# Strassen's algorithm for the feed-forward products, and modulation sums on the matmul engine, in a two-layer diffusion step

## The chip, the cores and the metric

One core of one Trainium2 chip runs the whole step as one program. The metric is the device time of a run in microseconds (us); the median of several runs is compared. Engines are named as the profile names them: PE is TensorE (matmuls), PEld its weight loads, DVE is VectorE, ACT is ScalarE, POOL is GpSimd and SP is SyncE, on whose queue this kernel issues all its DMA transfers.

## The reference, cut to what matters

Two layers work on 1152 tokens (1024 latent tokens and 128 context tokens) of 1024 features, all in float32. Each layer is a mixer (layer 0: a recurrence beside a pooling mixer, layer 1: latent attention) and then a feed-forward block. Ahead of both stands an RMS norm that is modulated with a scale and a shift from the conditioning vectors. The change concerns the feed-forward block and the modulation:

```python
def sq_relu_mlp(h, w1, w2):
    return jnp.square(jax.nn.relu(h @ w1)) @ w2      # 1024 -> 4096 -> 1024

m = jax.nn.silu(cond) @ w_mod + b_mod                # 1024 -> 6 * 1024, per layer and token kind
h = rms_norm(x, g) * (1 + scale) + shift
x = x + gate * sq_relu_mlp(h, w1, w2)
```

## The kernel before, in words

Activations lie feature-major: 128 features on the partitions, tokens along the free dimension. The 1152 tokens form three chunks of 384 (`CH`); the last holds the end of the latent tokens and the context tokens, which have their own modulation, so that vector operations on it come in two pieces (256 and 128 columns, `groups`, L236).

Float32 products keep their accuracy by splitting. `split` (L143) makes a rounded high part of an operand on ACT and the remainder, a subtraction, on DVE or POOL; `mm3` (L151 to L154) then issues three matmuls for each pair of tiles: high by high, high by low, low by high.

The feed-forward block is `ffn` (L707). It walks over 16 blocks of 256 hidden features. For each block two units of w1 and two of w2 (128 by 1024, 512 KB each) are loaded into `w_raw` by SP and split by ACT and DVE. `up` (L715) computes 2 x 128 hidden features of one chunk through `project` (L338, 24 matmuls into one PSUM bank), takes the relu on ACT (L719), the square on ACT for its high part and once more on POOL (L723), and the low part on DVE (L724). `down` (L729) multiplies with w2: for each of 8 output tiles 6 matmuls, and then DVE adds the bank, times the gate, to the activations `x` (`accum`, L335). A layer's block so issues 16 x 3 x 2 x 24 = 2304 matmuls in `up` and 16 x 3 x 8 x 6 = 2304 in `down`, each of 384 columns. In the last block `Tail` (L314) follows the additions with the squares and sums of the next norm, whose statistics (`Norm.stat`, L256) PE computes between other products, when `tick` (L302) says so.

During the feed-forward block of layer 0 the modulation of layer 1 is computed by `mod_slow` (L203), 384 of its 6144 columns at a time, in 16 parts: DVE multiplies rows of the weights by the conditioning and sums them up (L212, L214), PE adds over the partitions (L219) and transposes (L225). Layer 0's own modulation goes by `mod_steps` (L178), where PE does the products (L186): two matmuls of 512 columns for each slice of 128 rows, in a column group of the array of their own.

The order of PE's work is the order in which the program is written; all other engines and the DMA queue get theirs from a planner, except in the attention. A PSUM bank is one of eight that rotate (`bank`, L121). A buffer in a pool is handed on when its last reader is done. Attention, between the two feed-forward blocks, is computed head by head, and the change leaves it as it is.

## Time and profile before

| | |
|---|---|
| median of 3 runs | 2982.24 us (2981.44 to 2993.78) |
| span of the profiled execution | 2983.0 us |
| PE busy | 2838.5 us, 95% |
| DVE, ACT, POOL busy | 1868.8, 1130.8, 644.5 us |
| DMA | 188.22 MB, 63 GB/s on average |

The profiled execution is an execution of its own; only its span is given, and what lies around it is not listed. Busy time of PE is the union of its matmuls, which are pipelined: one of 384 columns is drawn 0.33 us long, yet the next starts long before it ends. The pace of PE is therefore read from start to start. A row of a timeline gives the start and the length in us, the engine, the line, and what is written from what.

### The profile page before, as it was taken

How to read it: one execution, taken by the hardware profiler on the slowest of the kernel's cores; microseconds unless marked ns; L12 is line 12 of the kernel's file. 1: busy time of each engine (PE TensorE's matmuls, PEld its weight loads, DVE VectorE, ACT ScalarE, POOL GpSimd, SP SyncE). 2: the span in 40 equal slices, each digit the busy share in tenths (PEclk: the TensorE clock that was granted, in tenths of full speed). 3: DMA queues.
4: the chain of work that ended last, by engine and by line, in shares of the span. 5: the costliest groups of instructions: out<-in, count | busy, mean ns of one | idle time of the engine just before them, and what ended most of it. 6: DMA issues, size and time to landing. Idle time of an engine off the chain costs nothing.

```text
span 2983.0 us, 43431 instructions
## 1 busy us (share of the span) xinstructions
PE 2838.5 (95%) x16896; PEld 2742.9 (92%) x16896; DVE 1868.8 (63%) x3400; ACT 1130.8 (38%) x2490; POOL 644.5 (22%) x600
## 2 busy tenths in 40 slices
PE   6898799999999999998999999999999999999997
PEld 3886699999999999988999999988999999999997
DVE  5469667776666666475777777775754454535355
ACT  3256333112121211255777777773521212121214
POOL 3444131001010100234323333340400101010003
PEclk7999899999999999999999999999999999999998
DMA  5233402222121222120000000023211111111101
GB/s 224 81 131 103 167 22 84 80 91 85 60 80 59 80 69 72 51 79 21 21 13 21 14 15 22 16 100 124 79 43 43 43 43 43 36 44 36 50 15 64
DMA packets 73415, 188.22 MB, mean 63 GB/s; under 512 B 9481, under 2 KB 40057, under 8 KB 72057
## 3 DMA queue, kind: packets, MB, share of 16 engines
q1 hardware_dynamic: 73208, 185.45, 18.3%
q8 instruction: 133, 2.18, 0.3%
q14 instruction: 74, 0.60, 0.1%
HBM read 168.67 MB, written 16.74 MB: 62 GB/s over the span
## 4 chain that ended last, share of the span: by engine, by line
PE 47%; ACT 3%; DVE 3%; issue 1%; DMA 1%; POOL 1%; SPq 0%; DVEq 0%; ACTq 0%; POOLq 0%
PE ps_b L152 10%; PE ps_b L153 10%; PE ps_b L154 10%; PE pS_o L978 3%; PE pS_t L960 3%; PE pS_s L152 3%; PE pS_s L154 2%; PE pS_s L153 2%; ACT aw_p L953 1%; PE pS_g L152 1%; PE pS_g L154 1%; PE pS_g L153 1%; ACT aw_ph L964 1%; DVE aw_mx L943 1%; DVE nt_xn L292 0%
## 5 line engine op out<-in xcount | busy, mean ns | idle before, releaser
L335 DVE SCALAR_TENSOR_TENSOR x_t<-ps_b,const_t,x_t 128x384 f32<-128x384 f32 (+2 forms) x1152 | 560.8, 513 | 274.9 <-PE ps_b L154 272.7
L152 PE MATMUL ps_b<-ffn_ah,wl_hlh 128*128 128x384 f32 x1488 | 498.5, 335 | 0.0
L154 PE MATMUL ps_b<-ffn_ah,wl_hll 128*128 128x384 f32 x1488 | 498.0, 335 | 0.0
L153 PE MATMUL ps_b<-ffn_al,wl_hlh 128*128 128x384 f32 x1488 | 497.9, 335 | 0.0
L723 POOL TENSOR_TENSOR ffn_r<-ffn_r 128x768 f32<-128x768 f32 x96 | 147.5, 1537 | 1437.6 <-ACT ffn_ah L722 1225.3
L148 ACT ACTIVATE wl_hlh<-w_raw 128x1024 fp32r<-128x1024 f32 x89 | 91.2, 1054 | 704.5 <-PE ps_b L153 694.8
L154 PEld LDWEIGHTS ps_b<-ffn_ah,wl_hll 128*128 128x128 f32 x1488 | 279.8, 188 | 0.0
L152 PEld LDWEIGHTS ps_b<-ffn_ah,wl_hlh 128*128 128x128 f32 x1488 | 279.8, 188 | 0.0
L153 PEld LDWEIGHTS ps_b<-ffn_al,wl_hlh 128*128 128x128 f32 x1488 | 279.8, 188 | 0.0
L719 ACT ACTIVATE ffn_r<-ps_b 128x384 f32<-128x384 f32 x192 | 93.1, 485 | 432.4 <-PE ps_b L154 432.1
L968 DVE TENSOR_TENSOR aw_pl<-pS_t,aw_ph 128x384 fp32r<-128x384 f32 (+1 forms) x400 | 200.2, 540 | 84.4 <-ACT aw_ph L964 78.8
L724 DVE TENSOR_TENSOR ffn_al<-ffn_r,ffn_ah 128x768 fp32r<-128x768 f32 x96 | 92.5, 963 | 243.3 <-POOL ffn_r L723 243.3
L953 ACT ACTIVATE aw_p<-pS_s,aw_nb 128x384 f32<-128x384 f32 (+1 forms) x400 | 224.6, 578 | 14.7 <-DVE aw_nb L947 14.0
L943 DVE TENSOR_REDUCE aw_mx<-pS_s 128x1 f32<-128x384 f32 (+1 forms) x400 | 203.2, 538 | 30.6 <-PE pS_s L154 29.5
L964 ACT ACTIVATE aw_ph<-pS_t 128x384 fp32r<-128x384 f32 (+1 forms) x400 | 173.6, 486 | 83.9 <-PE pS_t L960 83.5
L214 DVE SCALAR_TENSOR_TENSOR nt_acc<-nt_sq,const_t,nt_acc 128x384 f32<-128x384 f32 x224 | 160.9, 757 | 31.7 <-DMA nt_sq<-in_w_mod 30.2
L152 PE MATMUL ps_b<-ht0a_t,fw_w1h 128*128 128x384 f32 x480 | 164.0, 342 | 0.0
L152 PE MATMUL ps_b<-ht_t,fw_w1h 128*128 128x384 f32 x480 | 163.7, 341 | 0.0
L154 PE MATMUL ps_b<-ht0a_t,fw_w1l 128*128 128x384 f32 x480 | 162.6, 339 | 0.0
L152 PE MATMUL ps_b<-ht2a_h,fw_w1h 128*128 128x384 f32 x480 | 162.5, 339 | 0.0
L153 PE MATMUL ps_b<-ht2a_h,fw_w1h 128*128 128x384 f32 x480 | 162.5, 339 | 0.0
L154 PE MATMUL ps_b<-ht2a_h,fw_w1l 128*128 128x384 f32 x480 | 162.5, 339 | 0.0
(348 smaller groups left out, 6732.1 us busy)
## 6 DMA issues: line engine op xcount, KB each, us to landing
w_raw<-in_ffn SPq DMA_DIRECT2D x64, 512.0 KB, 4.3
w_raw<-in_l_ffn_w SPq DMA_DIRECT2D x64, 512.0 KB, 3.2
nt_sq<-in_w_mod SPq DMA_DIRECT2D x128, 192.0 KB, 2.4
w_raw<-in_w_mod SPq DMA_DIRECT2D x32, 512.0 KB, 3.8
w_raw<-in_w_in SPq DMA_DIRECT2D x18, 512.0 KB, 5.2
start_raw<-in_w_mod SPq DMA_DIRECT2D x16, 512.0 KB, 10.9
w_raw<-in_l_w_out SPq DMA_DIRECT2D x16, 512.0 KB, 4.1
n_t<-in_x SPq DMA_DIRECT2D x3, 1536.0 KB
```

The source lines that it names most:

```text
L152: mm(out, wh, hh, start=start, stop=False)
L153: mm(out, wh, hl, start=False, stop=False)
L154: mm(out, wl, hh, start=False, stop=stop)
L214: ve.scalar_tensor_tensor(acc[q], raw, sil[:, k, q:q + 1], acc[q], op0=OP.mult, op1=OP.add)
L335: done = ve.scalar_tensor_tensor(xv, b[:, a + o:e + o], gate[:, m, g:g + 1], xv, op0=OP.mult, op1=OP.add)
L719: act(r[:, j, :], b[:, :CH], AF.Relu)
L723: po.tensor_tensor(r, r, r, op=OP.mult)
L724: ve.tensor_tensor(al, r, ah.bitcast(F32), op=OP.subtract)
L943: ve.tensor_reduce(self.mx[:, i:i + 1], self.sc[i][0], axis=AX.X, op=OP.max)
L953: act(self.pt[i][:, :w], v, AF.Exp, bias=self.nb, accum_out=lsum[:, self.h, self.blk, i:i + 1])
L964: act(hi[g][:, :self.nks[g], j * P:(j + 1) * P], self.tp[g], AF.Copy)
L968: ve.tensor_tensor(lo[g][s_], self.tp[g], hi[g][s_].bitcast(F32), op=OP.subtract)
```

## The change

The tokens form four chunks of 288 (`Q`) from the output projection of layer 0 on (the attention's own blocks stay). Both feed-forward products are computed by one level of Strassen's algorithm in the form with seven products: token chunks in pairs (`g`, two pairs), features in halves. Seven right sides (`hp`: three of the activations themselves and four sums, slots 0 to 6) stand once for each pair in SBUF. For each of the 16 blocks the seven left sides come from four 128 x 512 quarters of the weights (`left_sides`, four subtractions or additions on POOL, in place, then seven splits). `up` issues for each of the seven products 4 x 3 matmuls of 288 columns, and combines the seven banks into four results with DVE, ACT and POOL; they are squared by one DVE operation. The squared results go to DRAM, three of them split (`ad`) and all four raw (`ar`).

Then the second product: blocks 0 and 1 (`PLAIN`) are multiplied as before, without Strassen, at two places where the activations change. The other 14 go in seven pairs; each product, chunk pair and output tile has 6 matmuls of 288 columns, and DVE adds the bank to an accumulator in SBUF. Right sides 0 to 2 are loaded from `ad` into three rotating buffers (`at`); 3 to 6 are summed by POOL from `ar` and split by ACT and DVE. At the end `collect` combines the accumulators, and `gated` adds them to `x`.

`mod_slow` goes. Layer 1's modulation is computed by `mod_steps` on PE, two slices after every fourth product of `up` in layer 0 (`mod_aside`). The norms and the output projection run over chunks of 288; some buffers are laid out anew.

```diff
+Q = 288
+NQ = T // Q
+PRODUCTS = (("A11", 0), ("S3", 5), ("A22", 4), ("S2", 3), ("A12", 1), ("S1", 6), ("S4", 2))
+LATE = (("A11", 0), ("A12", 1), ("S3", 5), ("A22", 4), ("S2", 3), ("S1", 6), ("S4", 2))
+PLAIN = (0, 1)
...
-    def mod_slow(l, r, s):
...
+    def enter(l, g, hp, scope):
+        hi, lo = hp
+        for k in range(4):
+            a = scope.t([P, 4, Q], tag="ac", bufs=2)
+            for j in range(2):
+                c = 2 * g + j
+                for i in range(2):
+                    kk = k + 4 * i
+                    for p, e, q in groups(c):
+                        r = a[:, PLACE[i, j], p:e]
+                        ve.scalar_tensor_tensor(r, x[c][:, kk, p:e], sc_ffn[l][:, kk, q:q + 1], nm.rs[c][:, p:e],
+                                                op0=OP.mult, op1=OP.mult)
+                        act(r, r, AF.Identity, bias=mod[l][:, 24 + kk, q:q + 1])
+            split(hi[:, 0:3, k, :], lo[:, 0:3, k, :], a[:, 0:3, :])
+            right_sides(a.unsqueeze(1))
+            split(hi[:, 3:7, k, :], lo[:, 3:7, k, :], a, eng=(ve, po)[k % 2])
+
+    def right_sides(a):
+        for o, p, q, op in ((2, 2, 3, OP.subtract), (3, 3, 0, OP.subtract), (0, 2, 0, OP.add), (1, 1, 0, OP.subtract)):
+            po.tensor_tensor(a[:, :, o, :], a[:, :, p, :], a[:, :, q, :], op=op)
+
+    def left_sides(quads, slots, low, order=PRODUCTS):
+        sub = lambda o, p, q, op=OP.subtract: po.tensor_tensor(o, p, q, op=op)
+        for name, _ in order:
+            out = []
+            for i, (a11, a12, a21, a22) in enumerate(quads):
...
+                h, lo = next(slots)
+                split(h, lo, src, eng=po if (name, i) in low else ve)
+                out.append((h, lo))
+            yield out
...
+    UP_LOW = {("A12", 0), ("S1", 0)}
+    DOWN_LOW = {(n, 1) for n, _ in PRODUCTS} | {("A12", 0), ("S4", 0)}
...
+        def up(g, s, cw):
+            a = fu.t([P, 6, Q], tag="ac", bufs=2)
+            place = lambda i: a[:, i, :]
+            bk = {}
+            for name, o in PRODUCTS:
+                (wh, wl), = next(cw)
+                b = bk[name] = bank()[:, :Q]
+                for k in range(4):
+                    mm3(b, wh[:, k * P:(k + 1) * P], wl[:, k * P:(k + 1) * P], hp[0][:, o, k, :], hp[1][:, o, k, :],
+                        k == 0, k == 3)
+                tick(1.5)
+                aside(fq)
+                plus = lambda e, to, p, q: e.tensor_tensor(place(to), p, place(q), op=OP.add)
+                if name == "A11":
+                    act(place(3), b, AF.Copy)
+                if name == "S2":
+                    plus(ve, 4, b, 3)
+                    plus(ve, 5, bk["S3"], 4)
+                    plus(ve, 1, bk["A22"], 5)
+                if name == "A12":
+                    plus(ve, 0, b, 3)
+                if name == "S1":
+                    act(place(2), b, AF.Copy)
+                    plus(po, 4, place(4), 2)
+                    plus(po, 2, place(5), 2)
+                if name == "S4":
+                    plus(ve, 3, b, 4)
+            ve.scalar_tensor_tensor(a[:, 0:4, :], a[:, 0:4, :], 0.0, a[:, 0:4, :], op0=OP.max, op1=OP.mult)
+            for p, e in ((0, 3), (3, 4)) if s in PLAIN else ((0, 3),):
+                t = fu.t([P, 3, 2, Q], F32R, tag="ah", bufs=2)[:, :e - p]
+                split(t[:, :, 0, :], t[:, :, 1, :], a[:, p:e, :])
+                nc.sync.dma_start(ad[s, g][:, p:e], t.bitcast(F32))
+            if s not in PLAIN:
+                nc.sync.dma_start(ar[s, g], a[:, 0:4, :])
...
+        for g in range(2):
+            if g:
+                enter(l, 1, hp, fu)
+                plain(0, raws, cycle(four(fq)), True, False)
+            for s in range(ns):
...
+                    cw = left_sides([up_quad(l, s, raws)], slots, UP_LOW)
+                up(g, s, cw)
...
+        for s in todo[::2]:
...
+            for name, o in LATE:
+                ws = next(cw)
+                for g in range(2):
+                    t = next(ats)
+                    if o > 2:
+                        n = 2 // len(right[g])
+                        for i, b in enumerate(right[g]):
+                            split(t[:, i * n:i * n + n, 0, :], t[:, i * n:i * n + n, 1, :],
+                                  b[:, :, o - 3, :])
+                    else:
+                        nc.sync.dma_start(t.bitcast(F32), ad[s:s + 2, g, :, o, :, :].rearrange("s p h q -> p s h q"))
+                    for m in range(4):
+                        b = bank()[:, :Q]
+                        for j in range(2):
+                            mm3(b, ws[j][0][:, m * P:(m + 1) * P], ws[j][1][:, m * P:(m + 1) * P],
+                                t[:, j, 0, :], t[:, j, 1, :], j == 0, j == 1)
...
+                            ve.tensor_tensor(to, b, to, op=OP.add)
+                    if end:
+                        collect(name, g)
...
+        plain(1, raws, ats, False, True)
...
+    def mod_aside(mq):
+        nonlocal count
+        count += 1
+        if count % 4:
+            return
+        s_ = next(mods1, None)
+        if s_:
+            if s_[0] not in mg1:
+                mg1[s_[0]] = mod_steps(1, s_[0], mq, 3)
+            next(mg1[s_[0]])
+            if s_[1] < KT // 2:
+                next(mg1[s_[0]])
```

## Rows read from the trace of the kernel before

**Rows 1.** The page: busy us of each engine, share of the span, instructions.

```profile
PE 2838.5 (95%) x16896; PEld 2742.9 (92%) x16896; DVE 1868.8 (63%) x3400; ACT 1130.8 (38%) x2490; POOL 644.5 (22%) x600
```

**Rows 2.** Windows over both feed-forward stretches: busy us of each engine, clock, DMA share, GB/s.

```profile
468.00:1289.00 821.00, 814.88 (x4650) 799.04 (x4650) 550.96 (x947) 169.07 (x258) 95.22 (x65) 1.00 0.22 73
2169.00:2961.00 792.00, 790.99 (x4526) 790.67 (x4526) 371.01 (x645) 165.48 (x249) 83.93 (x61) 1.00 0.11 39
```

**Rows 3.** Timeline of PE, layer 0 feed-forward: start, length; 68 matmuls of 384 columns apart.

```profile
900.04 0.33 PE L152 MATMUL ps_b<-ffn_ah,wl_hlh 128*128 128x384 f32 x1
...
911.83 0.33 PE L154 MATMUL ps_b<-ffn_ah,wl_hll 128*128 128x384 f32 x1
```

**Rows 4.** Timeline of PE, value projections: 23 matmuls of 256 columns apart.

```profile
1375.59 0.28 PE L152 MATMUL ps_b<-wkv_wkvh,kv_t 128*128 128x256 f32 x1
...
1378.35 0.27 PE L154 MATMUL ps_b<-wkv_wkvh,kv_t 128*128 128x256 f32 x1
```

**Rows 5.** Groups of DVE: line, form, count | busy us, mean ns | idle before.

```profile
L724 DVE TENSOR_TENSOR ffn_al<-ffn_r,ffn_ah 128x768 fp32r<-128x768 f32 x96 | 92.5, 963 | 243.3 <-POOL ffn_r L723 243.3
...
L506 DVE SCALAR_TENSOR_TENSOR ring_r<-ring_r,ring_r 128x1160 f32<-128x1160 f32 x8 | 10.6, 1352 | 0.0
...
L149 DVE TENSOR_TENSOR slots_wgl<-w_raw,slots_wgh 128x512 fp32r<-128x512 f32 x5 | 3.4, 682 | 3.9 <-ACT slots_wgh L148 3.9
```

**Rows 6.** Groups of POOL, as in group 5.

```profile
L149 POOL TENSOR_TENSOR att_t<-aw_qf,att_t 64x256 fp32r<-64x256 f32 x70 | 49.9, 730 | 0.0
L149 POOL TENSOR_TENSOR aw_ql<-aw_qf,aw_qh 128x384 fp32r<-128x384 f32 x47 | 47.4, 1008 | 194.6 <-ACT aw_qh L148 160.2 <-DMA dram_t<-aw_o 34.5
...
L884 POOL TENSOR_TENSOR aw_v<-vr_vr,aw_v 128x640 fp32r<-128x640 f32 x16 | 25.1, 1573 | 1.2
```

**Rows 7.** Source views of two DVE lines: ns min/median/max, first and last start.

```profile
L968 DVE TENSOR_TENSOR aw_pl<-pS_t,aw_ph x400: 272/548/559, 1404.5 to 2031.8; 128x384 fp32r<-128x384 f32 x128, 128x128 fp32r<-128x128 f32 x6
...
L1273 DVE TENSOR_TENSOR x_t<-x_t,nt_rs x16: 543/548/1371, 2946.0 to 2978.9; 128x384 f32<-128x384 f32 x16
```

**Rows 8.** Window over the attention, as in group 2.

```profile
1430.00:1940.00 510.00, 498.66 (x3578) 481.04 (x3576) 374.44 (x876) 387.43 (x1148) 167.54 (x213) 1.00 0.06 18
```

**Rows 9.** Timeline of DVE and POOL behind the last products.

```profile
2963.71 7.33 POOL L1273 TENSOR_TENSOR x_t<-x_t,nt_rs 128x384 f32<-128x384 f32 x6 [5.04 <-DVE nt_acc L254]
...
2965.04 2.61 DVE L1273 TENSOR_TENSOR x_t<-x_t,nt_rs 128x384 f32<-128x384 f32 x2
...
2967.58 2.61 DVE L254 TENSOR_TENSOR nt_acc<-nt_acc,nt_sq 128x384 f32<-128x384 f32 x2
```

**Rows 10.** Groups of ACT, as in group 5.

```profile
L719 ACT ACTIVATE ffn_r<-ps_b 128x384 f32<-128x384 f32 x192 | 93.1, 485 | 432.4 <-PE ps_b L154 432.1
L148 ACT ACTIVATE wl_hlh<-w_raw 128x1024 fp32r<-128x1024 f32 x89 | 91.2, 1054 | 704.5 <-PE ps_b L153 694.8 <-DMA w_raw<-in_w_in 8.9 <-DMA w_raw<-in_l_w_out 0.9
```

**Rows 11.** Timeline of PE around two slices of the layer 0 modulation.

```profile
204.98 0.34 PE L154 MATMUL ps_b<-ht_t,wl_hll 128*128 128x384 f32 x1
205.25 1.04 PE L186 MATMUL ps_b<-w_raw,const_t 128*2 128x512 f32 x8
206.22 0.44 PE L152 MATMUL ps_b<-slots_xh,slots_wgh 128*128 128x384 f32 x1
```

**Rows 12.** Groups of PE: sums and transposes of the layer 1 modulation.

```profile
L219 PE MATMUL ps_b<-nt_acc,const_t 128*2 128x384 f32 x64 | 13.0, 484 | 0.0
...
L225 PE MATMUL ps_b<-const_t,nt_rs 128*128 128x128 f32 x48 | 8.0, 275 | 2.0 <-ACT nt_rs L221 2.0
```

**Rows 13.** DMA issues: count, size, median us from issue to landing.

```profile
w_raw<-in_ffn SPq DMA_DIRECT2D x64, 512.0 KB, 4.3
w_raw<-in_l_ffn_w SPq DMA_DIRECT2D x64, 512.0 KB, 3.2
```

**Rows 14.** Window over the start, as in group 2.

```profile
0.00:30.00 30.00, 16.06 (x58) 2.95 (x62) 10.05 (x46) 8.79 (x16) 5.89 (x22) 0.85 0.94 364
```

More of the change, by code (lines that the diff above doesn't have):

```diff
@@ L628, in emit, with out_proj @@
     ht.close()
-    sw = Each("wo", "right")
-    pair = lambda: (sw.t([P, D], F32R), sw.t([P, D], F32R))
-    far = [pair() for _ in range(3)]
-    late = [pair()]
+    pair = lambda e: (e.t([P, D], F32R), e.t([P, D], F32R))
     xs_ = Each("x")
-    x = [xs_.t([P, KT, CH]) for _ in range(NC)]
+    x = [xs_.t([P, KT, Q]) for _ in range(NQ)]
     nsc = Scope("nt")
     nm = Norm(D, nsc)
-    tail = Tail(nm, x)
-    first = []
-    def ffn_up(l, f, **kw):
-        return [unit(A[f"ffn1_{l}"][2 * f + j], **kw) for j in range(2)]
-    def out_proj(rounds, gate, scope, tail, between, ready={}):
-        for r, (ks, weights, source) in enumerate(rounds):
+    def out_proj(rounds, gate, tail, between, ready={}):
+        for r, (ks, weights, source, scope, bufs) in enumerate(rounds):
             us = weights()
             yt = {}
-            for c in range(NC):
+            for c in range(NQ):
                 for k in ks:
@@ new lines, in left_first, with rights @@
+    def left_first(l):
+        cw = left_sides([up_quad(l, 0, cycle(from_wp))], slots_of([state["wl"]]), ())
+        return [next(cw) for _ in range(4)], cw
+    def rights(side="left"):
+        e = Each("rs_")
+        return e, (e.t([P, 7, 4, Q], F32R), e.t([P, 7, 4, Q], F32R))
+    ad = dr.t([DFF // 256, 2, P, 4, 2, Q])
+    ar = dr.t([DFF // 256, 2, P, 4, Q])
+    ro = Each("wo_")
+    rs0 = Scope("st0")
+    sw = Each("wo", "right")
+    far = [pair(sw) for _ in range(2)]
+    near = [pair(ro) for _ in range(2)]
@@ L1224, in emit @@
     xs_ = Each("x2")
-    x = [xs_.t([P, KT, CH]) for _ in range(NC)]
+    x = [xs_.t([P, KT, Q]) for _ in range(NQ)]
     nsc = Scope("nt2")
     nm = Norm(D, nsc)
-    tail = Tail(nm, x)
-    h0 = Each("ht2a")
-    hs0, t, hs2, hs3 = (h0.t([P, KT, CH], F32R, tag="h", bufs=1) for _ in range(4))
-    t = t.rearrange("p k t -> p (k t)")
-    early = t[:, 0:D], t[:, D:2 * D]
+    ro = Each("wo1_")
+    near = [pair(ro) for _ in range(2)]
     of = Scope("of", side="right")
```

467 lines of the change are left out of this document (272 added, 195 removed).

## The prediction

> **What bounds the kernel now.** I read the page first, then windows over the stretches that the change touches, then starts of single instructions. The page has PE busy for 95% of the span [rows 1]. In both feed-forward stretches PE works 815 of 821 us and 791 of 792 us at clock 1.00 (2.4 GHz), DVE 551 and 371, ACT under 170, POOL under 96, and the DMA queues 73 and 39 GB/s [rows 2]. So there the time is the number of matmuls times their pace. Sixty-eight steps of 384 columns take 11.79 us, 0.1734 us each [rows 3]; 23 steps of 256 columns take 2.76 us, 0.120 each [rows 4]. A layer's 2 x 2304 matmuls at 0.1734 make 799 us, 399.5 for each of the two products: what the stretches show. What the other engines do there is free as long as it keeps under PE.
>
> **Pace of 288 columns.** No row has this size. The ends are 0.120 (as for 256) and 0.1734 (as for 384); the line between them gives 0.120 + 0.25 x 0.0534 = 0.133 us, and I take it, since 288 is near 256 and matmuls of both sizes run back to back. The Trainium skill ("TensorE: Matmul & The Clock Gate", section Back-to-back issue gap) has columns over 2.4 GHz plus 2.5 ns, which would be 0.1225 here and take another 57 us from each layer; the rows show some 13 ns over the columns' own time at both sizes, so the measurement decides.
>
> **Matmuls.** First product: 2 pairs x 16 blocks x 7 products x 12 = 2688 per layer, 357.5 us of PE. Second: 7 block pairs x 7 x 2 x 4 x 6 = 2352, and 2 x 192 for the plain blocks: 2736, 363.9 us. Were PE alone the limit, each layer would fall from 799 to 721 us.
>
> **First product, the other engines.** I count one round: one block for one pair of chunks, 84 matmuls, 11.2 us of PE.
> - DVE, both inputs in SBUF: five low parts of 512 columns at 0.68, the squaring of 1152 columns at 1.35 (1160 took 1.352), the low part of 864 at 0.963 x 864/768 = 1.08 [rows 5]: 5.8 us. DVE, one input a PSUM bank: five additions of 288.
> - POOL: four sums and two low parts of 512 columns, midway between 1.008 for 384 and 1.573 for 640, 1.29 each, and two sums of 288, between 0.730 and 1.008, 0.80 each [rows 6]: 9.3 us. It is 3 us per chunk and block now, when it squares.
>
> Each fits alone. But the two hold each other up. A DVE addition from PSUM took 548 ns in the median and at most 559 [rows 7], in a stretch where POOL worked 168 of 510 us [rows 8]; a multiplication of the same width with both inputs in SBUF took 543 at least and 1371 at most [rows 7]. Behind the last products both have such work queued: six POOL operations of 384 columns take 7.33 us, 1.22 each against 1.008 alone, and the DVE operations of 384 between them 2.61 for two, 1.31 each against 0.54 (the line through 512 and 768 columns in [rows 5]) [rows 9]. One of each so takes 1.26 us where their own durations sum to 1.55: a factor of 0.81. In this round 5.8 + 9.3 = 15.2 us of such work become 12.3 us, already more than PE's 11.2. The five PSUM additions, 0.41 each (548 ns x 288/384), 2.1 in all, may run beside POOL or stand in DVE's queue behind an operation that waits for it. A round therefore takes 12.3 to 14.4 us; I take 13.0, a third of the way: three of the five come together, behind S2, and can lie under one or two POOL operations. PE then waits for low parts of weights and for banks.
>
> ACT has seven high parts of 512 columns, two copies and one high part of 864, about 6 us [rows 10]; it is not the bound.
>
> Layer 1: 32 x 13.0 = 416 against 399.5. Layer 0 has 24 pairs of modulation slices on PE too: from the last matmul before to the first behind one is 1.24 us, less the usual step 1.07 [rows 11], in all 26, and some 3 for six sets of transposes; 357.5 + 29 is still under 416, so they hide mostly under the held rounds; I add 4. **Term: +16.5 + 20.5 = +37 us** (at 12.3 -8, at 14.4 +127).
>
> **Second product.** A block pair has 336 matmuls, 44.7 us. DVE: 56 additions from PSUM, 23.0; five low parts of weights, 3.4; eight of 576 columns at some 0.75: 32.4. POOL: eight sums and nine low parts of 512, eight sums of 576 (some 1.43): 33.4. What the two hold against each other, 9.4 + 33.4 times 0.81, is 34.7. All stay under 44.7, so PE is the bound again: 2 x (363.9 - 399.5) = -71. What PE can wait for here are right sides from DRAM: three of seven products load two tiles of 590 KB, and with three buffers a load may start two tile uses ahead, 2 x 24 x 0.133 = 6.4 us. Loads of 512 KB land in 3.2 to 4.3 us [rows 13]. Such a load waits on SP for PE to release its buffer, and weights and stores queue behind it. All traffic is 8.0 MB per block pair, 179 GB/s, and 2.5 MB per round of the first product, 195; loads alone reached 364 [rows 14]. Between no wait and 1.5 us on each of 84 loads (126 us) I take 10, near the lower end, since a landing of 4.3 leaves 2 us over. **Term: -61.**
>
> **Modulation of layer 1.** Its PE sums and transposes were busy 13.0 + 8.0 us in layer 0's stretch [rows 12] and go: **-21**. DVE's products there hid under PE, and their going gives nothing by itself. The nt_sq loads, 128 of them, leave SP.
>
> **Four chunks elsewhere.** Both output projections go from 576 matmuls at 0.1734 to 768 at 0.133, +2.2 each, and layer 1's input projection from 432 to 576, +1.7: **+6**. Norm statistics work on smaller tiles beside products, as before: 0.
>
> **New seams.** Each layer forms the right sides of a chunk pair twice: POOL has 4 x 4 sums of 288 and two low parts of 1152, some 18 us, DVE about 13. Once the last two chunks of the output projection cover it, once the first plain block (192 matmuls, 25.5 us); the cover is as long as the work when the two engines hold each other. Where the second product begins, raw right sides are loaded and summed while four product-tile groups (12.8 us) run. Ends: 0 and 30 us for both layers; I take the middle: **+15**. The tail behind the last product keeps its steps: 0.
>
> **Sum:** 37 - 61 - 21 + 6 + 15 = -24 us. The profiled span, 2983.0, lies within 1 us of the median, 2982.24; from the median I predict 2958 us.
>
> **Rivals.**
> 1. *PE stays the bound throughout.* The factor 0.81 comes from operations of equal width in strict turn; if a freer order lets POOL work while DVE does its PSUM additions and waits, rounds come down to PE's own 11.2. For it: PE is at the limit now, and the factor rests on one stretch. Against it: 12.3 is already over. The first product is then 357.5 + 386.5 - 799 = -55 in place of +37: 2866 us.
> 2. *The two engines exclude each other for whole operations* (slower). Place: the rounds of the first product; price: 15.2 us a round. Then 2 x (32 x 15.2 - 399.5) = +174 in place of +37: 3095 us. It decides from 13.4 us a round, where 64 x 0.4 has used up the 24. For it: 1371 ns is one full wait behind a POOL operation. Against it: the strict turns cost 1.26 and not 1.55.
>
>    The Trainium skill ("SBUF — State Buffer", section SBUF: two separate sides) says that DVE operations with two SBUF inputs and GpSimd share a port pair by an exclusive lock for the whole instruction. By that rule this rival holds; the rows show the exclusion, but less than whole durations.
> 3. *Loads of right sides come late* by 1.5 us each, behind weights and stores on SP: 126 in place of 10: 3074 us. Against it: 179 GB/s is half of what was reached.
>
> That the matmuls don't get cheaper (0.1734 at 288 columns, 940 us a layer) the 256-column rows all but exclude.
>
> **Chances.** The forecast's case 0.50, rival 1 0.21, rival 2 0.18, rival 3 0.10, matmuls no cheaper 0.01. About 0.5%, 15 us, is what a measurement of this kernel can tell from no change. The forecast's own range is 2913 to 3010 (rounds of 12.3 to 13.8); of its 0.50, 0.27 is faster by more than 15 us, 0.14 within, 0.09 slower. With the rivals: faster 0.27 + 0.21 = 0.48, within 0.14, slower 0.09 + 0.18 + 0.10 + 0.01 = 0.38. The range reaches down over rival 1, to 2860, and up into the lower part of rivals 2 and 3, to 3050, which leaves out about 0.2.
>
> **What would show it.** In windows over the first product PE would be busy some 86%, with low parts of weights and PSUM additions on DVE as what it waits for, POOL near 70%, and DVE operations on SBUF far over 0.68 us; rounds repeat every 13 us. In the second product PE would be at 97% or more, steps of 0.133 us. Rounds of 11.2 show rival 1, of 15 rival 2; PE waiting for at<-dram rival 3. The forecast is wrong if rounds lie outside 12.3 to 13.8, if the 288-column step is not 0.13, or if the seams cost over 30 us.

## The result and the profile after

The changed kernel takes 3136.95 us (median of 4 runs, 3135.20 to 3138.84) against 2982.44 us for the kernel before, measured beside it: a ratio of 1.0514, interval 1.0496 to 1.0533. It is slower by 5%, outside the range, on the other side from the forecast. The profiled execution has a span of 3133.4 us. First the page, which answers to [rows 1]:

```profile
span 3133.4 us, 51531 instructions
...
PE 2788.9 (89%) x19232; PEld 2650.6 (85%) x19232; DVE 2314.1 (74%) x3820; ACT 1506.5 (48%) x3397; POOL 1854.7 (59%) x1444
```

PE's busy time fell by 50 us, but its share fell from 95 to 89%: it waits more. POOL worked 1210 us more. The windows over the two feed-forward blocks, from the first product of a block to its last (columns as in [rows 2]):

```profile
449.20:1349.80 900.60, 806.57 (x5684) 760.12 (x5683) 695.16 (x987) 359.12 (x686) 700.67 (x490) 0.94 0.57 194
2226.70:3114.50 887.80, 776.43 (x5468) 759.54 (x5466) 683.82 (x960) 357.60 (x692) 710.41 (x490) 0.93 0.49 164
```

Counted in the same way the blocks took 840.3 and 813.0 us before. They grew by 60.3 and 74.8 us; between them 859.8 became 876.9, and behind the last product 21.4 became 18.9. Nine tenths of the loss are inside the blocks.

Was it the matmul's price? In the timeline of PE there are 76 steps between these two products of the second product:

```profile
2876.01 0.29 PE L167 MATMUL ps_b<-fq_at,fw_hll 128*128 128x288 f32 x1
...
2886.03 0.30 PE L165 MATMUL ps_b<-fq_at,wl_hlh 128*128 128x288 f32 x1
```

10.02 us, 0.132 a step; over all 12,889 steps of this size the median is 0.133, just the value taken between [rows 3] and [rows 4]. (The Trainium skill, "TensorE: Matmul & The Clock Gate", section Back-to-back issue gap, has a formula for a single gap that gives 0.1225; the measurement decides here as it did for the two other sizes.)

Now the blocks cut into stages. A round is known by the start of every 84th matmul that reads `rs_t`, a block pair by every 336th that reads `fq_at`; plain blocks in the middle take in the wait ahead of them. Windows over the second stretch of layer 0 (first round, rounds 3 to 15), then over layer 1: plain blocks in the middle, first round and rounds 3 to 15 of the second stretch, first, middle five and last block pair, last plain blocks.

```profile
727.10:758.30 31.20, 16.67 (x94) 14.57 (x93) 14.80 (x20) 10.59 (x19) 23.62 (x17) 0.67 0.23 72
769.90:939.20 169.30, 156.04 (x1094) 152.02 (x1093) 137.76 (x151) 68.86 (x127) 145.95 (x99) 0.96 0.54 189
2451.20:2486.40 35.20, 28.69 (x196) 28.01 (x195) 31.20 (x54) 17.44 (x33) 18.70 (x16) 0.85 0.48 171
2486.40:2522.10 35.70, 16.15 (x86) 14.93 (x85) 19.18 (x21) 12.71 (x23) 25.08 (x20) 0.67 0.13 41
2533.30:2703.50 170.20, 153.87 (x1094) 150.11 (x1093) 129.02 (x152) 68.68 (x125) 144.85 (x99) 0.97 0.55 190
2715.90:2791.30 75.40, 57.48 (x337) 53.86 (x337) 35.38 (x32) 38.42 (x95) 65.02 (x52) 0.82 0.51 179
2791.30:3015.80 224.50, 222.50 (x1683) 221.67 (x1682) 186.53 (x344) 66.37 (x112) 173.92 (x120) 1.00 0.57 179
3015.80:3069.10 53.30, 46.53 (x339) 45.83 (x337) 51.41 (x74) 22.58 (x46) 36.23 (x21) 0.97 0.36 104
3069.10:3114.50 45.40, 34.65 (x222) 33.97 (x222) 39.20 (x69) 29.80 (x79) 30.71 (x22) 0.81 0.17 59
```

Read the long windows first. Thirteen rounds in 169.3 and 170.2 us are 13.0 and 13.1 each, five pairs in 224.5 us are 44.9 each: what the prediction said. Then the short ones: a first round takes 31 and 36 us, a first pair 75; there POOL is busy for most of the window, and PE's granted clock is 0.67 and 0.82. With both layers together the account is:

| stage (both layers) | measured us | at the forecast's rates | over |
|---|---|---|---|
| first rounds of four stretches: 31.5, 31.2, 29.8, 35.7 | 128.2 | 52.0 | +76 |
| the other 60 rounds | 793.4 | 784 | +9 |
| plain blocks in the middle | 70.8 | 51 | +20 |
| first block pairs | 144.7 | 89.4 | +55 |
| ten middle pairs | 448.8 | 457 | -8 |
| last block pairs | 107.4 | 89.4 | +18 |
| plain blocks at the end | 94.9 | 51 | +44 |

That is +214, where the term for new seams was +15. Against the 199 stand 34 us that the blocks of before also lost beyond their matmuls and modulation (840.3 + 813.0 - 2 x 799 - 21) and that the forecast kept. So the blocks miss it by 165 us, and with 13 us between the layers that is nearly the whole difference of 179. Of those 13 some 11 lie inside the attention, whose code is the same; why stays open.

What PE waits for in the first round of layer 1's second stretch (columns: waited for, us, times, longest), and its timeline:

```profile
PE ps_b L165 <- ACT rs_t L161: 15.3, 2, 11.8
PE ps_b L166 <- POOL rs_t L162: 3.7, 1, 3.7
```

```profile
2499.55 0.61 PE L165 MATMUL ps_b<-rs_t,wl_hlh 128*128 128x288 f32 x1 [11.83 <-ACT rs_t L161]
...
2501.53 0.44 PE L166 MATMUL ps_b<-rs_t,wl_hlh 128*128 128x288 f32 x1
2501.76 0.44 PE L167 MATMUL ps_b<-rs_t,wl_hll 128*128 128x288 f32 x1
...
2507.14 0.61 PE L165 MATMUL ps_b<-rs_t,wl_hlh 128*128 128x288 f32 x1 [3.49 <-ACT rs_t L161]
2511.49 0.61 PE L166 MATMUL ps_b<-rs_t,wl_hlh 128*128 128x288 f32 x1 [3.74 <-POOL rs_t L162]
```

The right sides are late. And after 11.83 us of idling PE's steps are 0.23 to 0.25 us apart, near twice 0.133. The granted clock of that stretch was 0.50, the lower of its two levels (1.2 GHz):

```profile
2499.50:2503.50 4.00, 3.47 (x12) 2.95 (x12) 2.98 (x3) 1.44 (x3) 2.68 (x3) 0.50 0.31 82
```

POOL around this round:

```profile
2478.12 6.50 POOL L676 TENSOR_TENSOR fu_ac<-fu_ac 128x288 f32<-128x288 f32 x6 [7.12 <-DVE rs_t L162]
...
2492.07 1.48 POOL L162 TENSOR_TENSOR fw_hll<-w_raw,fw_hlh 128x512 fp32r<-128x512 f32 x1
...
2500.66 3.26 POOL L676 TENSOR_TENSOR fu_ac<-fu_ac 128x288 f32<-128x288 f32 x3 [4.38 <-DVE rs_t L162]
...
2508.83 2.60 POOL L162 TENSOR_TENSOR rs_t<-fu_ac,rs_t 128x1152 fp32r<-128x1152 f32 x1
```

The right-side sums (L676) stand between weights of the coming rounds (L162, L680), and wait for DVE, which is at weights and additions too; the last low part ends at 2511.4, where the last of PE's waits ends.

### The profile page after: what moved, and what is told of

Its sections match the earlier page's. It is cut to its first block, busy times and chain, and to the rows that moved or that the text cites. A ratio compares the mean times of both kernels' runs of the same rounds, so it can differ in the third digit from the quotient of the medians.

```text
span 3133.4 us, 51531 instructions
## 1 busy us (share of the span) xinstructions
PE 2788.9 (89%) x19232; PEld 2650.6 (85%) x19232; DVE 2314.1 (74%) x3820; ACT 1506.5 (48%) x3397; POOL 1854.7 (59%) x1444
## 5 line engine op out<-in xcount | busy, mean ns | idle before, releaser
L165 PE MATMUL ps_b<-rs_t,wl_hlh 128*128 128x288 f32 x1104 | 340.8, 309 | 65.5 <-ACT rs_t L161 40.1
L166 PE MATMUL ps_b<-rs_t,wl_hlh 128*128 128x288 f32 x1104 | 337.4, 306 | 17.7 <-POOL rs_t L162 10.4
L167 PE MATMUL ps_b<-rs_t,wl_hll 128*128 128x288 f32 x1104 | 336.7, 305 | 3.0 <-DVE wl_hll L162 2.4
L902 DVE TENSOR_TENSOR acc_t<-ps_b,acc_t 128x288 f32<-128x288 f32 x656 | 276.7, 449 | 80.6 <-PE ps_b L167 78.7
L166 PE MATMUL ps_b<-fq_at,wl_hlh 128*128 128x288 f32 x1056 | 320.3, 303 | 14.1 <-DVE fq_at L162 14.1
L165 PE MATMUL ps_b<-fq_at,wl_hlh 128*128 128x288 f32 x1056 | 323.0, 306 | 8.9 <-DMA fq_at<-dram_t 4.0
L167 PE MATMUL ps_b<-fq_at,wl_hll 128*128 128x288 f32 x1056 | 317.7, 301 | 1.1 <-DVE wl_hll L162 1.1
L162 DVE TENSOR_TENSOR wl_hll<-w_raw,wl_hlh 128x512 fp32r<-128x512 f32 (+1 forms) x192 | 229.1, 1206 | 116.5 <-ACT wl_hlh L161 115.5
L165 PEld LDWEIGHTS ps_b<-rs_t,wl_hlh 128*128 128x128 f32 x1104 | 216.6, 196 | 81.7 <-ACT rs_t L161 42.6
L165 PE MATMUL ps_b<-fq_at,fw_hlh 128*128 128x288 f32 x736 | 223.6, 304 | 22.4 <-ACT fq_at L161 12.2
L167 PE MATMUL ps_b<-fq_at,fw_hll 128*128 128x288 f32 x736 | 223.5, 304 | 16.0 <-DVE fw_hll L162 9.8
L166 PEld LDWEIGHTS ps_b<-rs_t,wl_hlh 128*128 128x128 f32 x1104 | 216.7, 196 | 20.6 <-POOL rs_t L162 11.7
L1169 ACT ACTIVATE aw_p<-pS_s,aw_nb 128x384 f32<-128x384 f32 (+1 forms) x400 | 225.0, 579 | 15.8 <-DVE aw_nb L1163 14.8
L166 PE MATMUL ps_b<-fq_at,fw_hlh 128*128 128x288 f32 x736 | 223.9, 304 | 4.7 <-DVE fq_at L162 4.7
L166 PEld LDWEIGHTS ps_b<-fq_at,wl_hlh 128*128 128x128 f32 x1056 | 206.5, 196 | 16.2 <-DVE fq_at L162 16.1
L165 PEld LDWEIGHTS ps_b<-fq_at,wl_hlh 128*128 128x128 f32 x1056 | 206.2, 195 | 12.7 <-DVE acc_t L902 3.9
```

The lines of the kernel that those rows point to most:

```text
L162: eng.tensor_tensor(lo, src, hi.bitcast(F32), op=OP.subtract)
L165: mm(out, wh, hh, start=start, stop=False)
L166: mm(out, wh, hl, start=False, stop=False)
L167: mm(out, wl, hh, start=False, stop=stop)
L902: ve.tensor_tensor(to, b, to, op=OP.add)
L1169: act(self.pt[i][:, :w], v, AF.Exp, bias=self.nb, accum_out=lsum[:, self.h, self.blk, i:i + 1])
```

## The experiments

All runs are changes of the changed kernel. Times are set against its 3136.95 us; a run with an interval has it against the kernel before, which took 2979 to 2985 us in the median beside them. Runs that leave work out compute something else; they show only where time goes. A run of a single execution is marked.

**1. Are the rounds held by VectorE and POOL?** Run no_left_sums, the four sums of weight quarters left out in the first product:

```
-                if name == "S3":
+                if not sums:
+                    pass
+                elif name == "S3":
```

> The four sums of weight quarters in each round of the first product are left out (the quarters are used as they are), so 4 of POOL's operations of 128x512 go and nothing else. Theory (what VectorE and POOL do together, 15.2 us a round at 0.81, sets the rounds): steady rounds fall from 13.0 to TensorE's 11.2 to 11.6, the first rounds of the four stretches stay near 30, and the time falls by about 95 us, to 3040 (3020 to 3065). Rival 1 (rounds are set by a chain through the banks and the additions behind each product): rounds stay above 12.6 and the time above 3115. Rival 2 (the first rounds are long because of the left sides): the first rounds fall below 20 too, and the time below 3000.

3003.3 us, 134 less where 95 were expected: the other 60 rounds give back 93, and first rounds, first pairs and plain blocks some of the rest. Three stretches have rounds of 11.2 us (11.6 or 11.7 for the second round of two of them); the first, which has modulation, 13.1. Three of the first rounds stay, at 30.2, 32.1 and 31.0; layer 0's second falls to 22.4. The window over the inner rounds of the second stretch, and DVE's low part of 512 columns in it:

```profile
732.00:889.00 157.00, 157.00 (x1183) 157.00 (x1182) 113.49 (x172) 79.30 (x142) 66.31 (x58) 1.00 0.67 229
```

```profile
L162 DVE TENSOR_TENSOR wl_hll<-w_raw,wl_hlh 128x512 fp32r<-128x512 f32 x28 | 19.7, 739 | 5.4 <-ACT wl_hlh L161 5.0
```

PE 100%, at full clock. Run act_squares takes one DVE operation out instead:

```
-            ve.scalar_tensor_tensor(a[:, 0:4, :], a[:, 0:4, :], 0.0, a[:, 0:4, :], op0=OP.max, op1=OP.mult)
+            act(a[:, 0:4, :], a[:, 0:4, :], AF.Relu)
+            act(a[:, 0:4, :], a[:, 0:4, :], AF.Square)
```

> The squared ReLU of the first product goes from one operation of VectorE (128x1152, 1.26 us alone) to two of ScalarE, which is busy less than half the time; results stay the same. Theory (the summed work of VectorE and POOL, 15.2 us a round at 0.81 to 0.85 of it, sets the rounds): 1.3 us less of it makes the steady rounds 11.9 instead of 13.0, in the stretch with modulation 13.5 instead of 14.15, and the time falls by about 60 us, to 3075 (3055 to 3095). Rival (POOL alone sets the rounds, its ten operations one after another): rounds stay above 12.7 and the time above 3120.

3091.7 us; rounds 12.4, 12.5 and 12.3, with modulation 13.95. 1.35 us of DVE work less (the operation takes 1.33 us at least in the trace; 1.26 is in no run) gave 0.6 a round where 1.1 was expected: POOL alone doesn't set the rounds (rival), but neither do the two as one sum at a fixed rate. In the changed kernel's inner rounds both are stretched (groups of DVE and POOL; compare [rows 5] and [rows 6]), and PE waits for DVE's additions (layer 1's second stretch):

```profile
L162 DVE TENSOR_TENSOR wl_hll<-w_raw,wl_hlh 128x512 fp32r<-128x512 f32 x26 | 31.6, 1235 | 8.2 <-ACT wl_hlh L161 8.0
L756 DVE TENSOR_TENSOR fu_ac<-ps_b,fu_ac 128x288 f32<-128x288 f32 x62 | 26.8, 450 | 4.7 <-POOL fu_ac L756 4.0
...
L771 DVE SCALAR_TENSOR_TENSOR fu_ac<-fu_ac 128x1152 f32<-128x1152 f32 x13 | 20.8, 1602 | 1.8 <-POOL fu_ac L756 1.7
```

```profile
L680 POOL TENSOR_TENSOR w_raw<-w_raw,w_raw 128x512 f32<-128x512 f32 x18 | 28.2, 1570 | 0.6 <-DMA w_raw<-in_ffn 0.6
L162 POOL TENSOR_TENSOR wl_hll<-w_raw,wl_hlh 128x512 fp32r<-128x512 f32 x16 | 24.7, 1554 | 0.0
```

```profile
PE ps_b L165 <- DVE fu_ac L756: 15.9, 12, 2.4
```

DVE's low part of 512 columns takes 1.24 us, against 0.68, and with POOL's four sums gone 0.74: DVE's code is the same in both runs, so what stretches it is POOL's work. (Without the sums a weight's way to its low part is shorter too; no run separates that.) POOL's operations of that size take 1.55 to 1.57 in these rows, against 1.29 by the prediction's line; DVE's additions from PSUM 0.45 against 0.41, hardly touched.

**2. What is the first round waiting for?** Run enter_dve moves the right-side sums and POOL's low parts of `enter` to DVE:

```
-            right_sides(a.unsqueeze(1))
-            split(hi[:, 3:7, k, :], lo[:, 3:7, k, :], a, eng=(ve, po)[k % 2])
+            right_sides(a.unsqueeze(1), ve)
+            split(hi[:, 3:7, k, :], lo[:, 3:7, k, :], a)
```

> The sixteen right-side sums of each quarter entered, and the low parts that POOL made beside them, go to VectorE, so that nothing of this step is left on POOL. Theory (in the first rounds TensorE waits for POOL, where these sums queue between the left sides): first rounds fall from 31.5, 31.2, 29.8 and 35.7 us to about 20, the blocks in the middle from 35 to 31, and the time falls by about 45 us, to 3092 (3070 to 3110). Rival (it is the chain of dependent steps over two buffers, on whatever engine they are): first rounds stay within 5 us of what they were and the time within 15 us of 3137.

3113.0 us. First rounds 34.8, 21.3, 37.4 and 32.0: one falls by 10 and one by 4, two grow. What the time gained lies elsewhere (layer 0's block begins 10 us earlier, for one). So it is not POOL's queue alone, and neither theory has the time. Then the sums were left out altogether, run no_enter_sums:

```
-            right_sides(a.unsqueeze(1))
```

> The right-side sums of each quarter entered are left out; the seven right sides are still made, split and used, and nothing else changes. Theory (TensorE waits in the first rounds for the whole chain from the modulated quarter over two buffers to the last of the seven sides, of which the sums on POOL are a third): first rounds fall from 31.5, 31.2, 29.8 and 35.7 us to about 22, the blocks in the middle from 35 to 31, the time by about 40 us. Rival (the sums alone, queued on POOL between left sides, are the wait): first rounds fall to 14 to 16, as with eight quarter products, and the time by 70 us or more. Rival (neither: the splits of seven sides instead of four): first rounds stay above 27.

First rounds 13.8, 12.3, 12.4 and 14.0: the first rival, the sums (though, by enter_dve, not because they are on POOL). In their windows PE hardly waits:

```profile
718.50:730.80 12.30, 12.30 (x94) 11.27 (x93) 10.00 (x12) 6.20 (x13) 11.41 (x8) 1.00 0.44 134
2457.70:2471.70 14.00, 11.97 (x86) 11.26 (x85) 11.94 (x13) 4.78 (x10) 14.00 (x9) 1.00 0.20 56
```

But the time is 3090.8 us (one execution), 46 less, not the 76 that the first rounds lost. The rounds behind them pay 20 of it: the four stretches together fall from 921.5 to 865.2 us. In layer 0's second stretch the rounds 2 to 6 took 11.6, 11.2, 11.2, 11.2 and 14.9 us in the changed kernel, and 11.6, 11.2, 11.4, 13.1 and 15.1 here. That fits DVE and POOL working ahead while PE stands (not shown by a run of its own). In a stage that those two hold, a stall of PE is partly paid back later, and the removal of one is partly lost.

Why the sums cost so much can be read from the traces. From the first low part of a stretch's right sides to the last it takes 39.0, 50.1, 37.8 and 48.7 us in the changed kernel (in layer 1's first stretch from 2204.8 to 2242.5, while the first product starts at 2226.7), 34 to 45 us with the sums on DVE, and 20 to 26 without them. Each quarter goes through DVE and ACT (scale, bias and a first split), POOL's four sums, and a second split, over two buffers. In layer 1's first stretch POOL waits for DVE inside this chain; and in the 34 us ahead of it POOL is busy for only 4 (window, columns as in [rows 2]), so there no queue from earlier rounds stood in the way:

```profile
POOL en_ac L676 <- DVE rs_t L162: 7.3, 3, 4.5
```

```profile
2170.00:2204.00 34.00, 32.89 (x251) 32.46 (x251) 26.19 (x65) 16.90 (x41) 3.98 (x5) 1.00 0.19 54
```

How much of the 38 to 50 us is the chain, and how much other work of DVE and POOL between its steps, no run separates.

**3. The first pair of the second product.** Run first_pair moves low parts, and half of the right-side sums, to DVE:

```
-            cw = left_sides([down_quad(l, s + i, raws) for i in range(2)], slots, DOWN_LOW, LATE)
+            cw = left_sides([down_quad(l, s + i, raws) for i in range(2)], slots, DOWN_LOW if s != todo[0] else (), LATE)
-                    right_sides(t)
+                    right_sides(t, ve if s == todo[0] and g else po)
```

> In the first pair of the second product all nine low parts that POOL makes go to VectorE, and so do the right-side sums of the second column pair. Theory (POOL's queue is what the first pair waits for: busy 52.7 of 54 us there, against 36 of 45 later): the first pair falls from 69.2 and 75.4 us to about 52 in each layer, the later pairs stay at 44.3 to 45.4, and the time falls by about 40 us, to 3097 (3080 to 3110). Rival (the first pair waits for loads and for space that the first product hands over): the first pair stays within 4 us of 69 and 75, and the time at 3130 to 3140.

3115.9 us, 1.0445 [1.0417, 1.0474]; first pairs 61.1 and 61.1, half of what was expected. Run pair_no_sums leaves all 24 sums of that pair out (`right_sides(t)` and the four of `left_sides` only where `s != todo[0]`).

> In the first pair of the second product all sums on POOL are left out: sixteen of right sides and eight of weight quarters; low parts stay where they are. Theory (the first pair waits for POOL, which has the last round of the first product behind it and cannot begin earlier): first pairs fall from 69.2 and 75.4 us to about 48, against 61.1 with the low parts moved alone, and the time falls by 45 us. Rival (loads and handed-over space): first pairs stay above 60.

3092.6 us (one execution), 44 less; first pairs 49.7 and 53.6. Windows over layer 1's first pair, first_pair and then pair_no_sums:

```profile
2711.10:2772.30 61.20, 50.33 (x339) 48.84 (x338) 42.07 (x49) 37.88 (x96) 45.22 (x34) 0.92 0.62 222
```

```profile
2694.20:2747.80 53.60, 48.97 (x338) 47.94 (x337) 32.62 (x32) 38.00 (x95) 40.15 (x28) 0.90 0.71 252
```

With POOL's sums gone the pair is within 5 to 9 us of its 44.7, so it is the sums, not loads or space. In the changed kernel POOL, busy for 65.0 of the pair's 75.4 us, makes the sixteen right-side sums between weight parts; the pair begins at 2715.9, and these are the first of them and the last:

```profile
2732.04 0.81 POOL L676 TENSOR_TENSOR acc_t<-acc_t 128x288 f32<-128x288 f32 x1
...
2759.70 1.01 POOL L676 TENSOR_TENSOR acc_t<-acc_t 128x288 f32<-128x288 f32 x1
```

**4. Last pair and plain blocks.** Run plain_order issued the 16 squares of the norm's first two chunks behind the weights of the plain blocks.

> The squares and sums of the norm for chunks 0 and 1 are issued behind the weight parts and loads of the last plain blocks instead of ahead of them. Theory (the sixteen squares stand in ScalarE's and VectorE's queues ahead of the weights that the plain blocks need): the stretch of the plain blocks falls from 49.4 and 45.4 us to about 30 (25.5 is TensorE's own), the time by about 35 us, to 3102 (3085 to 3115). Rival (the weight parts wait for tiles that the last pair still reads, or for the additions of the sevenths, and the order of the squares does not matter): the stretch stays above 42, and the time within 8 us of 3137.

3136.8 us: nothing, as the rival said. Only PE's order follows the program; in this run's trace the squares stand among the weight parts as before. Run tail_early issued the squares inside the last pair, as each half chunk is complete.

> The squares and sums of the norm for chunks 0 and 1 are issued as each half of a chunk is complete, inside the last pair of the second product, instead of all behind it. Theory (TensorE, in its fixed order, stands at the norm's small products for the sums of the last chunks: 4.4 us in layer 0 and 14.7 in layer 1 in the last plain blocks): the plain blocks take 44 and 34 us instead of 49.4 and 45.4, and the time falls by about 15 us, to 3122 (3110 to 3130). Rival (the sums only move ahead of the additions of the last pair, which grows by as much): time within 6 us of 3137.

3159.5 us, 1.0577 [1.0551, 1.0603]: 22 us slower, a miss of both theories. The last pairs stay (54.0 and 53.3 us), the plain blocks take 54 and 56 us, and layer 1's first product begins 11.9 us later. In layer 0's plain blocks PE now stands in one wait for the norm's sums on POOL, where it waited 4.4 us before; why they come so late was not pursued.

```profile
PE ps_b L249 <- POOL nt_acc L239: 19.1, 1, 19.1
```

Run few_squares leaves 12 of the 16 squares and their sums out (`for m in (0, KT - 1)`), run no_collect the sums of the accumulators, their gates and their addition (`collect(name, g)` goes).

> Of the sixteen squares of the norm that stand between the last pair and the plain blocks twelve are left out, with their sums. Theory (TensorE stands at the norm's small products until the sums are done): plain blocks 49.4 and 45.4 to about 34, the time falls by 25 to 30 us. Rival (the wait is for the accumulators' sums behind the last pair, and for the weight parts): plain blocks stay above 43.

> The sums of the seven accumulators behind the last pair, the gates on them and their addition to the stream are left out; the norm, the plain blocks and the rest stay. Theory (the last pair and the plain blocks wait for this work on POOL, ScalarE and VectorE): last pairs fall from 54.2 and 53.3 us to 45, the plain blocks from 49.4 and 45.4 to about 36, the time by 35 us. Rival (only the last pair waits for it): plain blocks stay above 44, time down by 18 us or less.

few_squares (one execution): 3122.5 us, plain blocks 42.5 and 44.9, nearer to the rival. no_collect (one execution): 3106.1 us, last pairs 44.3 and 44.3, plain blocks 40.5 and 38.3. Windows over no_collect's last pair and plain blocks in layer 0:

```profile
1253.90:1298.20 44.30, 44.30 (x338) 44.30 (x337) 38.62 (x76) 15.41 (x28) 21.43 (x17) 1.00 0.46 133
1298.20:1338.70 40.50, 34.66 (x224) 32.96 (x223) 24.39 (x59) 13.36 (x32) 10.39 (x11) 0.87 0.36 126
```

The last pair's excess, and 7 to 9 us of the plain blocks, is the accumulators' work. With either left out, 13 to 19 us a layer over the 25.5 of PE remain in the plain blocks. In no_collect's, above, PE idles for only 5.8 us and is busy for 34.7 at a clock of 0.87; the cause of the rest stays open.

**5. Without the sums: eight products.** Run plain_up takes Strassen's algorithm out of the first product and keeps it in the second; relu and square go to ACT, as in act_squares:

```
-            for name, o in PRODUCTS:
-                (wh, wl), = next(cw)
-                b = bk[name] = bank()[:, :Q]
-                for k in range(4):
+            for i in range(2):
+                w = [next(cw) for _ in range(2)]
+                for j in range(2):
+                    b = bank()[:, :Q]
+                    for kk in range(8):
+                        wh, wl = w[kk // 4]
+                        o, k = PLACE[kk // 4, j], kk % 4
```

> The first product goes back to eight quarter products per pair of chunks (96 matmuls of 288 columns a round, 12.8 us), with no sums on either side; the second product keeps its sevenths. Theory (seams: in the first rounds TensorE waits for the right-side sums, and the steady rounds gain nothing on 12.8): steady rounds 12.8 to 13.0, first rounds 13 to 18 instead of 30 to 36, the plain blocks in the middle 27 instead of 35, and the time falls by about 95 us, to 3040 (3015 to 3065). Rival (the seams are made by the change of buffers, by chunks of 288 and by norm and modulation, whatever is multiplied): first rounds stay above 25 and the time above 3105.

3028.3 us, 1.0153 [1.0120, 1.0186]: 109 us less. Every round is 12.8 us but those with modulation, 14.8; first rounds 16.1, 12.8, 14.0 and 12.8; plain blocks in the middle 25.5. Its window over inner rounds:

```profile
732.00:899.00 167.00, 167.00 (x1256) 167.00 (x1255) 46.34 (x63) 74.69 (x132) 6.42 (x5) 1.00 0.56 197
```

Against the changed kernel's 13.0 the sevenths gained nothing even in steady rounds. But plain_up has two changes, and the run to hold it against is act_squares, which has the squares on ACT too: there the four first rounds take 129.5 us and the other 60 take 759.8, here 55.7 and 795.3. So the sevenths are worth 36 us in the steady rounds, and cost 74 in the first ones. First pairs fell by themselves, to 50.9 and 52.6; POOL is nearly idle ahead of them. But the middle pairs grew to 46.4 to 49.6, and there PE waits, in 190 us, for this:

```profile
PE ps_b L165 <- DMA fq_at<-dram_t: 8.9, 4, 2.8
```

The loads of right sides come late, as in rival 3; why here, and not in the changed kernel, was not pursued. A fourth buffer fits, since the results need less space without the sums: run best_a, with first_pair's and tail_early's edits.

```
-            a = fu.t([P, 6, Q], tag="ac", bufs=2)
+            a = fu.t([P, 4, Q], tag="ac", bufs=2)
-        four = lambda p: lambda: p.t([P, 2, 2, Q], F32R, tag="at", bufs=3)
+        four = lambda p: lambda: p.t([P, 2, 2, Q], F32R, tag="at", bufs=4)
```

> The first product as eight quarter products with a smaller result buffer (as in the run before), the first pair of the second product with its low parts and half of its sums on VectorE, the norm's sums issued early, and four buffers instead of three for the loaded right sides (TensorE waited up to 2.8 us for one of these loads in the pairs of the run with eight quarter products, which took 48 us instead of 45). Theory (these are separate costs and add up): pairs 45 us, 12 of them 3 us shorter, first pairs 48, plain blocks 10 us shorter, time 3028 - 36 - 6 - 15 = 2971 (2955 to 2995). Rival (the pairs of 48 us come from the order of the loads, not from the number of buffers): pairs stay at 47 to 49, and the time at 3000 to 3015.

2987.7 us, 1.0010 [0.9992, 1.0027]; eleven of the twelve pairs ahead of the last 44.3 to 44.4 us, one 45.3, so it was the buffers and not the order of the loads. The plain blocks, expected 10 us shorter, take 55 and 49, with a wait like tail_early's (19.0 us). Run best_b, without the early squares and with the norm's products later in PE's order:

```
-(po, ve)[c // 3], (12, 16, 8, 14)
+(ve, po, po, ve)[c], (16, 22, 8, 14)
```

> The last combination (eight quarter products first, first pair relieved, four buffers for the loaded right sides) without the early squares, but with the norm's small products of chunks 0 and 1 set 4 and 6 us later in TensorE's order and chunk 0's sums on VectorE. Theory (early squares cost 22 us alone, and TensorE stood 10 to 11 us a layer at the norm's products): 2987.6 - 22 - 8 = 2958 (2945 to 2972). Rival (the squares cost only with the sevenths in both products): 2975 to 2990.

2987.3 us, 1.0009 [0.9998, 1.0019]: no gain, the rival's range. The later norm moved the wait: the blocks are 10 us shorter, but from the last product to the end of the span it is 24 us, against 16 in best_a, and between the layers 5 more. Run best_d, two of the accumulators' sums on DVE (`add(ve, "A22", ...)`, `add(ve, "S4", ...)`):

> As best_b, with two of the four large sums of each column pair behind the last pair (128x1152) by VectorE instead of POOL (POOL took 3.4 us for one). Theory (POOL's sums stand ahead of the norm's): last pair and plain blocks 5 to 8 us shorter a layer, the time 10 to 15 us below best_b. Rival (VectorE and POOL hold each other up, so that moving work from one to the other gives nothing): within 5 us of best_b.

2997.0 us, 1.0039 [1.0027, 1.0051]: 10 us slower than best_b, a miss of both theories. From layer 1's last plain blocks to the end PE waits 20.7 us for the norm's sums on DVE, against 15.1 in best_b.

**6. The modulation.** Run best_c is best_b with layer 1's modulation sums on DVE and only the sum over partitions on PE:

```
+                    ve.scalar_tensor_tensor(acc[q], raw, sil[:, k, q:q + 1], acc[q], op0=OP.mult, op1=OP.add)
...
+                mm(pm[g:g + 2, :], ones[:, 0:2], acc[q][:, h * 512:(h + 1) * 512], start=True, stop=True,
+                   tile_position=(0, g))
```

> As best_b, with the modulation sums of layer 1 by VectorE (rows of 1024 times a scalar, added up over the slices) and only their sum over the partitions by TensorE, over both stretches of layer 0's first product. Theory (with 12.8 us of products in a round TensorE has no room, so the 48 slices cost all of their 32 us there, and VectorE is idle over half the round): the rounds with modulation fall from 14.8 to 13.2 us, those of the second stretch go from 12.8 to 13.2, and the time falls by 20 us against best_b. Rival (VectorE's larger operations hold up the weight parts): rounds above 13.8 in both stretches and no gain.

2966.4 us, 0.9939 [0.9924, 0.9954], 21 less than best_b. Windows over inner rounds of the first stretch, best_b and then best_c:

```profile
463.10:670.40 207.30, 207.30 (x1549) 184.69 (x1545) 54.91 (x89) 83.99 (x148) 0.00 (x0) 1.00 0.82 285
```

```profile
458.40:642.20 183.80, 183.80 (x1381) 180.72 (x1381) 101.97 (x125) 82.08 (x145) 0.00 (x0) 1.00 0.77 265
693.10:876.90 183.80, 183.80 (x1381) 180.72 (x1381) 97.55 (x121) 82.42 (x145) 2.59 (x2) 1.00 0.72 252
```

14 rounds in 207.3 and in 183.8 us, PE busy throughout in both: with the slices on PE a round is 2.0 us longer than 12.8, with the sums on DVE some 0.3, in both stretches. Run best_e has best_c's edits but the norm as the changed kernel has it.

> As best_c (eight quarter products, modulation sums by VectorE, first pair relieved, four buffers) with the norm's waits and engines as the changed kernel has them. Theory (later norms only move the wait behind the plain blocks: the tail grew from 16 to 24 us with them): 2966.4 - 5 = 2961 (2952 to 2970). Rival (the waits inside the plain blocks return, 8 us a layer): 2975 to 2985.

2954.0 us, 0.9898 [0.9879, 0.9917]: faster than both kernels, though by only 1.0% than the one before. Its feed-forward blocks:

```profile
448.40:1259.90 811.50, 792.58 (x5922) 784.21 (x5922) 566.06 (x869) 351.93 (x677) 291.40 (x195) 0.99 0.63 214
...
2135.50:2932.80 797.30, 780.59 (x5850) 778.34 (x5850) 450.07 (x751) 353.95 (x689) 290.00 (x195) 0.99 0.54 182
```

## Why the prediction was wrong

**Right.** The step of 288 columns (0.133). Steady rounds: 13.0 to 13.3 where no modulation runs, between the ends 12.3 and 14.4. That it is VectorE and POOL holding each other is shown: leave POOL's four sums out and each round is PE's 11.2 and DVE's low part falls from 1.24 to 0.74 us; take 1.35 us from DVE and the round is shorter too. The size was in part luck: a factor of 0.81 on the whole sum would have given 1.1 us for act_squares, and it gave 0.6. Two of the signs were off: the forecast had PE 86% and POOL 70% busy, and they were 92 and 86%; POOL's operations grow with the hold too. By the rule in the Trainium skill ("SBUF — State Buffer", section SBUF: two separate sides), the lock for whole instructions, rounds would have been 15.2, rival 2; they weren't. Steady pairs: 44.9 against 44.7, and loads late by next to nothing (PE waited 5.1 us for them in the whole span), so rival 3 was wrong here.

**Wrong: "New seams: +15."** The step said that the right sides of the last two chunks are formed under the output projection or the first plain block, and that "raw right sides are loaded and summed while four product-tile groups (12.8 us) run", between 0 and 30 us in all. Measured over the forecast's rates: first rounds +76, first pairs +55, last pairs +18, plain blocks +64. This includes the wait at the middle blocks (+20), which goes with plain_up (25.5 us) and was not split further. Three things failed in it.
- It took the forming of the right sides as a block of work, 18 us of POOL and 13 of DVE, that a cover of 25 us hides. It is a chain of steps over two buffers on engines that also have other work, and it took 38 to 50 us from its first low part to its last; in layer 1's first stretch that first one came 22 us ahead of the first product. Leaving out `enter`'s sums takes all of the 76 us from the first rounds. At the first pair the cover of 12.8 us was too short by far: POOL ended the last of the sixteen sums 45 us into the pair, and leaving out its 24 sums takes 41 of the 55.
- It had no term for the end of the second product: the sums of seven accumulators, their gates, and the norm behind them: 62 us, 35 of which go with no_collect. "The tail behind the last product keeps its steps: 0" looked only behind that product.
- It left out the clock. PE fell to its lower level in long waits; the mean was 0.67 to 0.77 in the first rounds, 0.88 and 0.82 in the first pairs. Counted by the steps at 0.24 us, that is 2.0 to 3.2 us in each first round and 3.4 and 8.4 in the first pairs, some 22 of the 214.

**Wrong by size: the modulation.** The prediction says that they "hide mostly under the held rounds; I add 4". The price was right, 29 against 32 measured (best_b's first stretch against its second); but rounds with slices took 14.05 us and not 13.0, 16 us over the stretch. A round that DVE and POOL hold at 13.0 does have PE time free, but in gaps that aren't where the slices stand in PE's fixed order (argued from the sizes; the runs show only that half of the 2.0 us a round showed in the changed kernel, three quarters in act_squares, and nearly all in no_left_sums). The slices themselves, to compare with [rows 11]:

```profile
L199 PE MATMUL ps_b<-fq_at,const_t x184: 591/592/593, 473.3 to 696.7; 128*2 128x512 f32 x184
```

The gain that the change aimed at, 71 us of PE in the second product, is there in the middle pairs (448.8 us for ten, where the same 20 blocks took 20/16 of 399.5, 499, before), and it is spent at both ends of the product. best_e shows what is left when the first product goes back to eight quarter products and the modulation leaves PE: 28 us of 2982.

## What to carry to other kernels

An algorithm that trades matmuls for additions moves the bound to the engines that add. Price its steady state by what those engines take together, not by each alone. Then price each boundary by the length of the chain that must end before the first product there can start, from the moment at which its input is ready, and not by the summed busy time of the engines: here 31 us of work, held together 25, took 38 to 50. Ask the same of the end of the product. Leaving out the sums, a run that takes one line, tells how much of a stall they are, and moving them to another engine whether it is that engine's queue; but where those engines hold the stage, expect to get back less than the stall (46 of 76 us here).

## What was not expected of the hardware

A squaring of 1152 columns moved from DVE to ACT shortened a round by 0.6 us, half its own time, where the factor of 0.81 would have given 1.1: the two engines' mutual hold is not a fixed rate on the sum of their work. (Leaving out four POOL sums of 512 columns shortened it by 1.8; there PE became the limit, so their full price isn't known.) And behind waits of 4 to 12 us PE ran stretches of a few microseconds at the lower clock, at 0.24 us a step instead of 0.133: 19 to 30 steps in each first round of 84 products.
